# Two quarters of tokens together through three Strassen products in a hybrid decoder layer

## The chip, the cores and the metric

The kernel runs on one core of one Trainium2 chip. The metric is the device time of one execution in microseconds (us); lower is better. A core has a matrix engine (PE, with its weight loads listed as PEld), a vector engine (DVE), a scalar engine (ACT), GpSimd (POOL, hardly used here) and SyncE (SP), whose queue issues every DMA of this kernel.

## The reference

One decoder layer over 2048 tokens of width 1024, in float32. Biases, the convolutions' insides and the recurrence are left out here.

```python
h = rms_norm(x, mix_norm_g)
lru_x, lru_gate, conf_a, conf_b = split(h @ w_in, 4)            # 4 x 512
y_lru = rg_lru(causal_dwconv(lru_x, 4 taps)) * gelu(lru_gate)
c = causal_dwconv(conf_a * sigmoid(conf_b), 31 taps)
c = silu(layer_norm(c))
x = x + concat([y_lru, c]) @ w_out                              # output projection
h = rms_norm(x, xa_norm_g)
k, v = split(rms_norm(mem, mem_norm_g) @ w_kv, 2)               # 256 memory tokens, 4 heads
p = softmax((h @ w_q) . k / 16)                                 # per head
x = x + (p . v) @ w_o
h = rms_norm(x, ffn_norm_g)
g, u = split(h @ w_up, 2)                                       # 2 x 3072
x = x + (gelu(causal_dwconv(g, 3 taps)) * u) @ w_down
return rms_norm(x, final_norm_g)
```

## The kernel before

**Number format.** Each float32 operand is split into a high part `hi`, rounded for the matrix engine's fast float32 mode, and the rest `lo` (`split`: one ACT copy, one DVE subtraction). A product is three matrix multiplies, hi by hi, hi by lo and lo by hi (`mm3`). A multiply takes a 128x128 stationary and a 128x512 moving operand.

**Tokens.** The 2048 tokens are worked on in four quarters of 512 (`TT`), each of four blocks of 128 (`NTB`). Per quarter there are three tasks. `mixer(q)` does the first normalisation, the input projection, the convolutions (`conf`: 30 DVE taps for each of four channel blocks) and the recurrence (`lru`). `normed(q)` does the layer norm of the convolved half (`conf_out`). `attend(q)` does the rest up to the input of the feed-forward.

**attend(q).** It has three products with a 1024x1024 right side, each through `project_tokens`: for each half of the 1024 output columns it holds four PSUM banks, one for each token block, and adds eight k-blocks of 128 into them. The left operands lie with the contracted dimension on the partitions, so that the 128x128 pieces of them are the stationary side. The three are

- output projection: left `Y` and `L` (the two halves of the mixer's result), right `W_out`; each bank is added on DVE to the residual `xs`, and ACT squares it for the next normalisation;
- scores: left the transposed residual `xa`, right `A_rows`, which `memory_a` makes beforehand as w_q times the keys, so that h @ w_q and the keys are one product; `softmax` reads each bank (maximum on DVE, exponential and scaling on ACT), with the normalisation's factor in the exponential's scale;
- values: left the transposed probabilities `pt`, right `VO_rows`, which `memory_vo` makes as the values times w_o; again added to the residual, squared, normalised, transposed and stored in DRAM (`xn_kept`).

The right sides are kept in DRAM as hi and lo (`Rows`) and read again for each quarter.

**Feed-forward.** `up` and `Down` work on halves of 1024 tokens and use one level of Strassen's method in Winograd's form: seven products of half-size blocks in place of eight, with the sums S1 to S4 and T1 to T4 of the blocks of either side made on DVE. `HalfX` makes the combinations of the normalised tokens: `X[0]` needs quarters 0 and 1 alone, and its first five operands are made ahead by the task `first`, once `started[3]` is set. `feed_forward` (the task `tail`) waits for `attended[3]`, the end of the last values product.

**Order.** The program is written by tasks (Python generators). `drive` keeps a clock of estimated PE time and steps the first due task of the list `TURNS`, so an earlier place in the list is a higher priority; a task that yields a number comes due that many us later, one that yields a task waits for it. The constants `MIX_PACE`, `ATT_PACE` and so on are such pauses. After that `Program.schedule` orders each engine's instructions by estimated costs and due times and with a limited number of buffers (84 tiles of 128x512 in SBUF, 8 PSUM banks), given out in program order. The order of each engine and of SP's queue is then fixed in the program, and each engine runs its own in that order.

Of the kernel before, what the change touches and what calls it, by code (L numbers as in the profile page):

```python
# [417 lines left out]
def hybrid_layer(  # L418
# [41 lines left out]
    def ps():  # L460
        return pr.new("ps", name="ps")
# [347 lines left out]

    def conf_out(C, Y):  # L810
        s = block_sum(C, False)
        yield LN_SUM
        p = ps()
        matmul(p[:], ones[:], s[:], start=True, stop=True)
        for c in range(NC4):
            V("tensor_tensor", C[c][:], C[c][:], p[:], op=ALU.subtract)
        ss = block_sum(C, True)
        yield LN_SQ
        r = wide_rstd(ss, 1.0)
        for c in range(NC4):  # L820
            w = vec["v512"][:, c, :]
            V("scalar_tensor_tensor", C[c][:], C[c][:], w[:, I_LG : I_LG + 1], r[:], op0=ALU.mult, op1=ALU.mult)
            ACT(C[c][:], C[c][:], AF.Silu, bias=w[:, I_LB : I_LB + 1])
            hi, lo = pair("y")
            split(C[c][:], hi, lo)
            Y.append((hi, lo))

    def lru(q, X, L, row, pace):
        for c in (0, 2):
# [46 lines left out]
            for j in range(2):  # L876
                ge = tmp("gelu")
                ACT(ge[:], scaled("gelu", pg[j], row)[:], AF.Gelu_apprx_tanh)
                V("tensor_tensor", ge[:], H[j][:], ge[:], op=ALU.mult)
                hi, lo = pair("y")  # L880
                split(ge[:], hi, lo)
                L.append((hi, lo))
# [158 lines left out]
    started = [Task(None) for _ in range(NQ)]  # L1041
    attended = [Task(None) for _ in range(NQ)]
    x2_kept = Kept("x2", NQ * NTB * 2, F32)
    xn_kept = Kept("xn", NQ * NK, F32)
# [121 lines left out]
    def normed(q, ready, wait):  # L1166
# [4 lines left out]
        Y = []  # L1171
        yield from conf_out(C, Y)
        mixed[q] = Y, L

    def attend(q, ready):
# [24 lines left out]

        yield from turned(xs, take)
        yield mem_a
        prob = [[], []]
# [251 lines left out]
    class Down:  # L1455
# [18 lines left out]
        def operand(self, c, key, i):  # L1474
# [13 lines left out]
            return self.s[at]  # L1488

        def gather(self, c, n):  # L1490
            if (c, n) in self.ready:
# [3 lines left out]
            for i in range(KD):  # L1495
# [3 lines left out]
                L.append((hi, lo))  # L1499
                at = wd_at(c, bkey, i)  # L1500
                R.append(self.given[c, n][i] if (c, n) in self.given else (wd_kept.get(at, None, "wh"), wd_kept.get(at + 1, None, "wl")))
            self.R = R
# [23 lines left out]
        def run(self, last=None):  # L1526
            for c in self.order:
# [20 lines left out]
                if not self.h:  # L1548
# [5 lines left out]
                    self.add(pa, 1, 0)  # L1554

    def finish(h, acc):
        g = []
# [40 lines left out]
    EARLY, VO_WAIT, V_LATE, Z_COPIED = 5, 2, 500, (0, 1)  # L1598
    MIX_WAIT, MIX_TURN, LN_SUM, LN_SQ, GATES = (0, 10, 0, 0), 9, 2, 0, 4
    MIX_PACE, ATT_PACE = (1, 4, 4, 4), ((0, 4, 1), (0, 2, 6), (0, 1, 0), (0, 2, 4))  # L1600
    PAUSE = 2
    MEM_WAIT, VO_LATE, ATT_TURN, FFN_TURN, X_PACE, T_PACE = 12, 10, 1, (6, 16, 6, 100), 10, 11

    NORMED = [lambda: ([m[0]], 105), lambda: ([attended[0]], 35), lambda: ([attended[1]], 140), lambda: ([m[3], n[2]], 115)]
    ATTEND = [lambda: [n[0]], lambda: [n[1]], lambda: [n[2]], lambda: [n[3], attended[2]]]
    TURNS = lambda: [later, n[2], m[0], mem_a, m[1], n[1], n[3], a[0], n[0], mem_vo, m[2], first, a[3], a[2], a[1], m[3], first_t, tail]
    X = [HalfX(h) for h in range(NH)]
# [29 lines left out]
    for q in range(NQ):  # L1637
        m[q].gen = mixer(q, m[q - 1] if q else None)
        n[q].gen = normed(q, *NORMED[q]())
        a[q].gen = attend(q, ATTEND[q]())  # L1640
    later.gen, mem_a.gen, mem_vo.gen = setup_later(), memory_a(), memory_vo()
    first_t.gen, first.gen, tail.gen = X[0].kept(n[3], T_PACE), first_x(), feed_forward()
    tasks.extend(TURNS())
# [33 lines left out]
```

## Time and profile before

| | |
|---|---|
| Median of 3 runs | 2469.93 us (2469.36 to 2470.13) |
| The profiled execution, its own time | 2470.41 us |
| Its span, first to last instruction | 2468.5 us |
| PE busy | 2450.5 us, 99% |
| DVE busy | 1825.8 us, 74% |
| ACT busy | 1171.0 us, 47% |
| DMA | 543.70 MB, mean 220 GB/s |

In the groups of the profile a line names an engine, an operation, the tiles it writes and reads, the shapes, the count, busy time and the mean in ns of one, and the idle time just before with what ended it. Windows list a stretch, then the busy time of each engine with its number of instructions, the granted PE clock (1.00 is full), the DMA share and GB/s. Nearly all instructions carry line 394, since one function emits them all; tiles tell them apart.

### The profile page before, as it was taken

To read this page: it belongs to the slowest core of one execution; us is meant where nothing else is said; L and a number is where in the kernel's file an instruction comes from. 1 tells how busy PE (TensorE), PEld (TensorE's weight loads), DVE (VectorE), ACT (ScalarE), POOL (GpSimd) and SP (SyncE) were. 2 spreads that over 40 slices of the span, in tenths; PEclk is the share of its full clock that TensorE was granted. 3 is DMA by queue.
4 is the path that set the end of the run, shared out by engine and by line. 5 is a ranking of instruction groups with operands and counts; after the bars stand their busy time and mean duration, and the time that the engine had idled before them with its cause. 6 is when DMAs were issued, how large, how long until landed. Compare 5 with 4: busy or idle time off the path is not lost. (4 is left out here: it accounts for less than half of the span.)

```text
span 2468.5 us, 32772 instructions
## 1 busy us (share of the span) xinstructions
PE 2450.5 (99%) x11212; PEld 2037.8 (83%) x11212; DVE 1825.8 (74%) x3041; ACT 1171.0 (47%) x2041; POOL 0.7 (0%) x6
## 2 busy tenths in 40 slices
PE   9999999999999999999999999999999999999998
PEld 7898888888888788888888888888888888888887
DVE  7999993697279532369888887987886675667666
ACT  6762664366416543465545455555454432224223
POOL 0000000000000000000000000000000000000000
PEclk9999999999999999999999999999999999999999
DMA  9598676677456748777654545444542387779675
GB/s 318 209 302 320 214 256 236 214 257 257 150 174 238 250 158 293 260 254 249 234 196 151 181 165 178 166 165 163 179 145 94 120 279 263 247 253 357 234 253 177
DMA packets 327741, 543.70 MB, mean 220 GB/s; under 512 B 31580, under 2 KB 109404, under 8 KB 327574
## 3 DMA queue, kind: packets, MB, share of 16 engines
q1 hardware_dynamic: 327574, 541.60, 63.9%
q8 instruction: 89, 1.46, 0.2%
q14 instruction: 78, 0.64, 0.1%
HBM read 396.78 MB, written 144.70 MB: 219 GB/s over the span
## 5 line engine op out<-in xcount | busy, mean ns | idle before, releaser
L394 PE MATMUL ps<-Xh,wh 128*128 128x512 f32 x1344 | 523.4, 389 | 0.0
L394 PE MATMUL ps<-Xh,wl 128*128 128x512 f32 x1344 | 523.0, 389 | 0.1
L394 PE MATMUL ps<-Xl,wh 128*128 128x512 f32 x1344 | 522.9, 389 | 0.0
L394 DVE SCALAR_TENSOR_TENSOR conv<-cb,v,conv 128x512 f32<-128x512 f32 x480 | 339.6, 743 | 2.8 <-ACT conv L394 0.9
L394 PEld LDWEIGHTS ps<-Xh,wl 128*128 128x128 f32 x1344 | 252.2, 188 | 53.2 <-DVE wl L394 0.6
L394 PEld LDWEIGHTS ps<-Xh,wh 128*128 128x128 f32 x1344 | 252.3, 188 | 52.7 <-DVE up L394 0.4
L394 PEld LDWEIGHTS ps<-Xl,wh 128*128 128x128 f32 x1344 | 252.3, 188 | 52.2
L394 PE MATMUL ps<-wl,hidh 128*128 128x512 f32 x672 | 261.4, 389 | 0.0
L394 PE MATMUL ps<-wh,hidh 128*128 128x512 f32 x672 | 261.4, 389 | 0.0
L394 PE MATMUL ps<-wh,hidl 128*128 128x512 f32 x672 | 261.4, 389 | 0.0
L394 DVE TENSOR_TENSOR acc<-acc,ps 128x512 f32<-128x512 f32 x192 | 129.4, 684 | 143.8 <-PE ps L394 141.2
L394 PE MATMUL ps<-xh,wh 128*128 128x512 f32 x512 | 202.7, 396 | 0.8 <-ACT xt L394 0.8
L394 PE MATMUL ps<-xh,wl 128*128 128x512 f32 x512 | 199.4, 389 | 0.0
L394 PE MATMUL ps<-xl,wh 128*128 128x512 f32 x512 | 199.3, 389 | 0.0
L394 ACT ACTIVATE wh<-s 128x512 fp32r<-128x512 f32 x192 | 119.3, 627 | 111.9 <-DVE s L394 85.6
L394 ACT ACTIVATE wh<-raw 128x512 fp32r<-128x512 f32 x208 | 127.1, 626 | 85.0 <-PE ps L394 40.1
L394 DVE TENSOR_TENSOR wl<-raw,wh 128x512 fp32r<-128x512 f32 x208 | 141.0, 684 | 24.6 <-ACT wh L394 22.9
L394 DVE TENSOR_TENSOR wl<-s,wh 128x512 fp32r<-128x512 f32 x192 | 131.1, 686 | 29.0 <-ACT wh L394 20.2
L394 ACT ACTIVATE u<-ps 128x512 f32<-128x512 f32 x144 | 85.9, 597 | 138.9 <-PE ps L394 137.9
L394 PEld LDWEIGHTS ps<-wh,hidh 128*128 128x128 f32 x672 | 126.1, 188 | 26.2
L394 PEld LDWEIGHTS ps<-wl,hidh 128*128 128x128 f32 x672 | 126.1, 188 | 26.2
L394 PEld LDWEIGHTS ps<-wh,hidl 128*128 128x128 f32 x672 | 126.1, 188 | 26.1
(206 smaller groups left out, 4246.0 us busy)
## 6 DMA issues: line engine op xcount, KB each, us to landing
raw<-in_w_up_dram SPq DMA_DIRECT2D x96, 512.0 KB
wh<-w_down SPq DMA_DIRECT2D x164, 256.0 KB
wl<-w_down SPq DMA_DIRECT2D x164, 256.0 KB
wh<-w_in SPq DMA_DIRECT2D x96, 256.0 KB
wl<-w_in SPq DMA_DIRECT2D x96, 256.0 KB
hid<-cv SPq DMA_DIRECT2D x48, 512.0 KB
h<-hid SPq DMA_DIRECT2D x96, 256.0 KB
w_down<-wh SPq DMA_DIRECT2D x84, 256.0 KB
```

Of the source, the lines that this page charges most:

```text
L394: getattr(e, name)(*[resolve(a) for a in args], **{k: resolve(a) for k, a in kw.items()})
```

## The change

Quarters 2 and 3 (`FOLDED`) no longer have an `attend` each. A task `attend_pair` takes them together, 1024 tokens, once the layer norms of both and the attention of quarter 1 are done, and each of its three products is one level of Strassen (`Folded`, built on `Down`): seven steps of 512x512x512. The combined right sides T1 to T4 of `W_out`, `A_rows` and `VO_rows` are made by a new task `fold_weights` (`Folds`), stored in DRAM as float32, and split into hi and lo when they are read. The left operands stay in float32 and are split, plain or combined, at each step. The scores come in two parts that are added before the softmax. The factor of the second normalisation is applied before the transposes, no longer in the exponential. The residual after the output projection goes to DRAM and comes back for the values. `started[3]` is set at step 4 of the last product. The pauses and the list of priorities have new values.

```diff
-    def conf_out(C, Y):
+    def conf_out(q, C, Y):
...
+            if q in FOLDED:
+                Y.append(C[c])
+                continue
             hi, lo = pair("y")
             split(C[c][:], hi, lo)
...
                 V("tensor_tensor", ge[:], H[j][:], ge[:], op=ALU.mult)
+                if q in FOLDED:
+                    L.append(ge)
+                    continue
                 hi, lo = pair("y")
                 split(ge[:], hi, lo)
...
+    class Folds:
+
+        def __init__(self, rows, name):
+            self.rows, self.t, self.done = rows, Kept(name, 4 * KH, F32), Task(None)
+
+        def block(self, k, half):
+            if self.rows.w is not None:
+                t = tmp("wd")
+                pr.dma(t[:], self.rows.w[k * P : (k + 1) * P, half * TT : (half + 1) * TT])
+                return t
+            hi, lo = self.rows.get(k, half)
+            t = tmp("wd")
+            V("tensor_tensor", t[:], hi[:].f32(), lo[:].f32(), op=ALU.add)
+            return t
+
+        def prepare(self, wait):
+            for i in range(KH):
+                b11, b12 = self.block(i, 0), self.block(i, 1)
+                t1 = combine("t", b12[:], b11[:], ALU.subtract)
+                self.t.put(KH + i, t1[:])
+                yield wait
+                b22 = self.block(KH + i, 1)
+                t3 = combine("t", b22[:], b12[:], ALU.subtract)
+                t2 = combine("t", b22[:], t1[:], ALU.subtract)
+                self.t.put(2 * KH + i, t3[:])
+                self.t.put(i, t2[:])
+                yield wait
+                t4 = combine("t", self.block(KH + i, 0)[:], t2[:], ALU.subtract)
+                self.t.put(3 * KH + i, t4[:])
+                del b11, b12, b22, t1, t2, t3, t4
+                yield wait
+            self.done.done = True
+
+        def weight(self, key, i):
+            if key[0] == "B":
+                return self.rows.get((int(key[1]) - 1) * KH + i, int(key[2]) - 1)
+            t = self.t.get(T_KEYS.index(key) * KH + i)
+            hi, lo = pair("w")
+            split(t[:], hi, lo)
+            return hi, lo
+
+    class Folded(Down):
+
+        STEPS = (("A11", "B11"), ("A12", "B21"), ("S2", "T2"), ("S1", "T1"), ("S4", "B22"), ("S3", "T3"), ("A22", "T4"))
+
+        def __init__(self, src, folds, add):
+            self.src, self.folds, self.put = src, folds, add
+            self.raw, self.s, self.ready, self.given = {}, {}, {}, {}
+
+        def hid(self, c, kq, th, i):
+            return self.src[th, kq][i]
+
+        def weight(self, c, key, i):
+            return self.folds.weight(key, i)
+
+        def step(self, n, banks, start, into):
+            L, R = self.gather(0, n)
+            for tb in range(NTB):
+                if len(banks) == tb:
+                    banks.append(ps())
+                ts = slice(tb * P, (tb + 1) * P)
+                with together():
+                    for i in range(KH):
+                        mm3(banks[tb][:], L[i][0][:, ts], L[i][1][:, ts], R[i][0][:], R[i][1][:], start and i == 0, i == KH - 1, skip_group_check=True)
+                for th, half, last in into:
+                    self.put(th, tb, half, banks[tb], last)
+                yield 0
+
+        def run(self, before, after):
+            pa, pb, pc, pd = [], [], [], []
+            steps = (
+                (pa, True, ((0, 0, False),)),
+                (pb, True, ((0, 0, True),)),
+                (pa, False, ((0, 1, False),)),
+                (pc, True, ((1, 1, False),)),
+                (pc, False, ((0, 1, True),)),
+                (pa, False, ((1, 1, True), (1, 0, False))),
+                (pd, True, ((1, 0, True),)),
+            )
+            for n, (banks, start, into) in enumerate(steps):
+                yield from before(n)
+                yield from self.step(n, banks, start, into)
+                after(n)
+
+    def attend_pair(ready):
+        for t in ready:
+            yield t
+        q0 = FOLDED[0]
+        me = a[q0]
+        src = {}
+        x1_kept = Kept("x1", 4 * NTB, F32)
+
+        def nothing(n):
+            return ()
+
+        def residual(load, store, st):
+            acc = {}
+
+            def add(th, tb, half, bank, last):
+                at = (th, tb, half)
+                if at not in acc:
+                    acc[at] = load(th, tb, half)
+                t = acc[at]
+                V("tensor_tensor", t[:], t[:], bank[:], op=ALU.add)
+                if last:
+                    st[th].add(tb, half, t[:])
+                    store(th, tb, half, t)
+
+            return acc, add
+
+        def normalise(acc, th, st, wait, take):
+            yield wait
+            r = st[th].rstd()
+            ys = []
+            for tb in range(NTB):
+                row = []
+                for half in range(2):
+                    t = tmp("xn")
+                    ACT(t[:], acc[th, tb, half][:], AF.Copy, scale=r[:, tb : tb + 1])
+                    row.append(t)
+                ys.append(row)
+            yield PAIR_TURN
+            yield from turned(ys, take)
+
...
+        def after1(n):
+            if n in (4, 6):
+                th = n // 6
+                posts[th] = spawn(normalise(acc, th, st1, PAIR_WAIT[0], take_xa(th)), me)
+
+        yield F_out.done
+        yield from Folded(src, F_out, add).run(nothing, after1)
+        del acc, add
+
+        yield mem_a
+        yield F_a.done
+        psrc, score = {}, {}
+        prob = {}
+        turns = []
+
+        def soften(th, tb, half, bank, last):
+            at = (th, tb, half)
+            if not last:
+                t = score[at] = tmp("score")
+                ACT(t[:], bank[:], AF.Copy)
+                return
+            t = score.pop(at)
+            V("tensor_tensor", t[:], t[:], bank[:], op=ALU.add)
+            prob.setdefault((th, half), []).append(softmax(t, M ** -0.5, -(M ** -0.5)))
+
+        def turn_raw(th, half):
+            yield PAIR_WAIT[1]
+            for j in range(4):
+                p = ps()
+                with together():
+                    for tb in range(NTB):
+                        transpose(p[:, tb * P : (tb + 1) * P], prob[th, half][tb][:, j * P : (j + 1) * P], ident[:])
+                t = tmp("pt")
+                ACT(t[:], p[:], AF.Copy)
+                psrc.setdefault((th, half), []).append(t)
+                if j % 2:
+                    yield 0
+
+        def before2(n):
+            if n == 0:
+                yield posts[0]
+            if n == 2:
+                yield posts[1]
+
+        def after2(n):
+            for at in {4: ((0, 0), (0, 1)), 5: ((1, 1),), 6: ((1, 0),)}.get(n, ()):
+                turns.append(spawn(turn_raw(*at), me))
+
+        yield from Folded(xsrc, F_a, soften).run(before2, after2)
...
+        def before3(n):
+            if n == EARLY_AT:
+                started[NQ - 1].done = True
+            if n == 0:
+                yield turns[0]
+            if n == 1:
+                yield turns[1]
+            if n == 2:
+                yield turns[2]
+                yield turns[3]
+
+        def after3(n):
+            if n in (4, 6):
+                th = n // 6
+                finals.append(spawn(normalise(acc2, th, st2, PAIR_WAIT[2 + th], take_xn(th)), me))
+
+        yield from Folded(psrc, F_vo, add2).run(before3, after3)
+        for th in range(2):
+            attended[q0 + th].done = True
+        for t in finals:
+            yield t
+
+    def fold_weights():
+        for f, ready, wait in zip((F_out, F_a, F_vo), FOLD_AT(), FOLD_PACE):
+            for t in ready:
+                yield t
+            yield from f.prepare(wait)
+
     EARLY, VO_WAIT, V_LATE, Z_COPIED = 5, 2, 500, (0, 1)
-    MIX_WAIT, MIX_TURN, LN_SUM, LN_SQ, GATES = (0, 10, 0, 0), 9, 2, 0, 4
-    MIX_PACE, ATT_PACE = (1, 4, 4, 4), ((0, 4, 1), (0, 2, 6), (0, 1, 0), (0, 2, 4))
+    MIX_WAIT, MIX_TURN, LN_SUM, LN_SQ, GATES = (1, 13, 0, 0), 6, 7, 1, 4
+    MIX_PACE, ATT_PACE = (0, 4, 6, 4), ((0, 3, 0), (0, 0, 6), (7, 1, 1), (4, 0, 6))
     PAUSE = 2
-    MEM_WAIT, VO_LATE, ATT_TURN, FFN_TURN, X_PACE, T_PACE = 12, 10, 1, (6, 16, 6, 100), 10, 11
-
-    NORMED = [lambda: ([m[0]], 105), lambda: ([attended[0]], 35), lambda: ([attended[1]], 140), lambda: ([m[3], n[2]], 115)]
-    ATTEND = [lambda: [n[0]], lambda: [n[1]], lambda: [n[2]], lambda: [n[3], attended[2]]]
-    TURNS = lambda: [later, n[2], m[0], mem_a, m[1], n[1], n[3], a[0], n[0], mem_vo, m[2], first, a[3], a[2], a[1], m[3], first_t, tail]
+    MEM_WAIT, VO_LATE, ATT_TURN, FFN_TURN, X_PACE, T_PACE = 0, 11, 1, (5, 0, 17, 5), 6, 2
+
+    FOLDED = (2, 3)
+    PAIR_WAIT, PAIR_TURN, FOLD_PACE = (1, 0, 9, 15), 5, (15, 6, 40)
+    EARLY_AT = 4
+    FOLD_AT = lambda: ([turned_x[0]], [mem_a, turned_x[1]], [mem_vo])
+    F_out, F_a, F_vo = Folds(W_out, "t_out"), Folds(A_rows, "t_a"), Folds(VO_rows, "t_vo")
+
+    NORMED = [lambda: ([m[0]], 111), lambda: ([attended[0]], 33), lambda: ([m[2]], 2), lambda: ([m[3], n[2]], 0)]
+    ATTEND = [lambda: [n[0]], lambda: [n[1]]]
+    TURNS = lambda: [later, m[0], first_t, m[3], n[1], first, mem_a, fold, m[1], a[0], n[0], mem_vo, m[2], n[2], n[3], a[1], a[2], tail]
...
-        a[q].gen = attend(q, ATTEND[q]())
+        if q not in FOLDED:
+            a[q].gen = attend(q, ATTEND[q]())
+    a[3] = a[2]
+    a[2].gen = attend_pair([n[2], n[3], attended[1]])
+    fold = Task(fold_weights())
     later.gen, mem_a.gen, mem_vo.gen = setup_later(), memory_a(), memory_vo()
-    first_t.gen, first.gen, tail.gen = X[0].kept(n[3], T_PACE), first_x(), feed_forward()
+    first_t.gen, first.gen, tail.gen = X[0].kept(a[1], T_PACE), first_x(), feed_forward()
```

More of the change, by code (lines that the diff above doesn't have):

```diff
@@ L1042, in hybrid_layer @@
     attended = [Task(None) for _ in range(NQ)]
+    turned_x = [Task(None) for _ in range(NQ)]
     x2_kept = Kept("x2", NQ * NTB * 2, F32)
@@ L1171, in normed @@
         Y = []
-        yield from conf_out(C, Y)
+        yield from conf_out(q, C, Y)
         mixed[q] = Y, L
@@ L1201, in attend @@
         yield from turned(xs, take)
+        turned_x[q].done = True
         yield mem_a
@@ L1488, in operand @@
             return self.s[at]
+        def weight(self, c, key, i):
+            at = wd_at(c, key, i)
+            return wd_kept.get(at, None, "wh"), wd_kept.get(at + 1, None, "wl")
         def gather(self, c, n):
@@ L1499, in gather @@
                 L.append((hi, lo))
-                at = wd_at(c, bkey, i)
-                R.append(self.given[c, n][i] if (c, n) in self.given else (wd_kept.get(at, None, "wh"), wd_kept.get(at + 1, None, "wl")))
+                R.append(self.given[c, n][i] if (c, n) in self.given else self.weight(c, bkey, i))
             self.R = R
@@ L1554, in run @@
                     self.add(pa, 1, 0)
+    T_KEYS = ("T2", "T1", "T3", "T4")
+    class Folds:
[34 more added lines that the diff above has]
+            return hi, lo
@@ new lines, in hybrid_layer, with weight @@
+    class Folded(Down):
[5 more added lines that the diff above has]
+            return self.src[th, kq][i]
+        def weight(self, c, key, i):
+            return self.folds.weight(key, i)
[26 more added lines that the diff above has]
+                after(n)
@@ new lines, in attend_pair, with load_one, operands, take_xa @@
+    def attend_pair(ready):
[32 more added lines that the diff above has]
+            yield from turned(ys, take)
+        def load_one(th, tb, half):
+            t = tmp("x1")
+            r0 = (q0 + th) * TT + tb * P
+            pr.dma(t[:], x[0, r0 : r0 + P, half * TT : (half + 1) * TT])
+            return t
+        def operands(th):
+            Y, L = mixed[q0 + th]
+            src[th, 0], src[th, 1] = L, Y
+        operands(0)
+        operands(1)
+        st1 = [Stats(), Stats()]
+        acc, add = residual(load_one, lambda th, tb, half, t: x1_kept.put((th * NTB + tb) * 2 + half, t[:]), st1)
+        xsrc, posts = {}, [None, None]
+        def take_xa(th):
+            def take(k, p):
+                t = tmp("xa")
+                ACT(t[:], p[:], AF.Copy, scale=vec["v1024"][:, k, G_XA : G_XA + 1])
+                xsrc.setdefault((th, k // KH), []).append(t)
+            return take
+        def after1(n):
[40 more added lines that the diff above has]
+        yield from Folded(xsrc, F_a, soften).run(before2, after2)
+        xsrc.clear()
+        yield mem_vo
+        yield F_vo.done
+        st2 = [Stats(), Stats()]
+        acc2, add2 = residual(
+            lambda th, tb, half: x1_kept.get((th * NTB + tb) * 2 + half, None, "acc"),
+            lambda th, tb, half, t: x2_kept.put(((q0 + th) * NTB + tb) * 2 + half, t[:]),
+            st2)
+        finals = []
+        def take_xn(th):
+            def take(k, p):
+                t = tmp("xt")
+                ACT(t[:], p[:], AF.Copy, scale=vec["v1024"][:, k, G_FFN : G_FFN + 1])
+                xn_kept.put((q0 + th) * NK + k, t[:])
+            return take
+        def before3(n):
[17 more added lines that the diff above has]
+            yield t
```

## The prediction

> **What bounds the kernel now.** I read the page first (busy shares, the slices), then busy time by stages, then the matrix-multiply groups, then what PE waited for.
>
> ```profile
> PE 2450.5 (99%) x11212; PEld 2037.8 (83%) x11212; DVE 1825.8 (74%) x3041; ACT 1171.0 (47%) x2041; POOL 0.7 (0%) x6
> PE   9999999999999999999999999999999999999998
> DVE  7999993697279532369888887987886675667666
> ACT  6762664366416543465545455555454432224223
> PEclk9999999999999999999999999999999999999999
> ```
> ```profile
> 0.00:100.00 100.00, 94.70 (x461) 79.96 (x462) 81.60 (x169) 68.28 (x121) 0.70 (x6) 1.00 0.87 304
> 100.00:350.00 250.00, 249.01 (x1244) 212.95 (x1243) 245.41 (x417) 139.91 (x238) 0.00 (x0) 1.00 0.78 267
> 350.00:600.00 250.00, 249.65 (x1179) 207.46 (x1179) 180.99 (x315) 133.17 (x237) 0.00 (x0) 1.00 0.68 230
> 600.00:830.00 230.00, 226.27 (x1054) 187.06 (x1053) 159.67 (x277) 118.33 (x217) 0.00 (x0) 1.00 0.61 210
> 830.00:1095.00 265.00, 264.31 (x1240) 219.58 (x1239) 104.12 (x190) 116.04 (x264) 0.00 (x0) 1.00 0.68 238
> 1110.00:2010.00 900.00, 899.97 (x3971) 744.83 (x3970) 739.39 (x1150) 448.67 (x687) 0.00 (x0) 1.00 0.51 173
> ```
>
> Columns: window, length, busy time of PE, PEld, DVE, ACT, POOL, granted clock, DMA share, GB/s. PE is the bound from end to end: idle 18 us of 2468.5, only 0.7 us of it between 830 and 1095, where the last two quarters attend. DVE is full in bursts (the convolutions of the mixers) and 39% busy from 830 to 1095; ACT is 44% there. A change must take matrix work from PE, or it gains nothing; what it adds to DVE and ACT is free only while PE has something else to do.
>
> **What a multiply costs.**
>
> ```profile
> L394 PE MATMUL ps<-wh,yh 128*128 128x512 f32 x256 | 100.3, 392 | 0.0
> L394 PE MATMUL ps<-wh,xah 128*128 128x512 f32 x256 | 100.1, 391 | 0.0
> L394 PE MATMUL ps<-wh,pth 128*128 128x512 f32 x256 | 101.2, 395 | 0.3
> ```
> ```profile
> 1003.00:1028.00 25.00, 25.00 (x112) 1.00 0.64 196
> ```
>
> The groups are the output projection (y), the scores (xa) and the values (pt), each the first of three terms (high by high, high by low, low by high). So each product has 768 multiplies, 192 for a quarter. Their mean of 390 ns is not what one costs: in the stage from 1110 to 2010, 3971 fit into 899.97 us, 0.2266 us each, and a stretch of attention (25 us, 112) goes at the same pace. The records overlap; the pitch is the price.
>
> The Trainium skill (TensorE: Matmul & The Clock Gate, "Wait — 56ns, not 53.3ns?") gives the start-to-start time of a warm multiply as N / 2.4 GHz plus about 2.5 ns, 215.7 ns at N = 512. By it the multiplies saved below would be worth 31.1 us and not 32.6; the trace's pitch is 5% longer, so I use the trace.
>
> **The change part by part.** *PE, removed.* Two quarters by the plain form: 2 x 192 = 384 multiplies for a product. By one level of Strassen: 7 steps x 4 token blocks x 4 k-blocks x 3 terms = 336. Three products: 3 x 48 = 144 fewer, 144 x 0.2266 = **32.6 us off PE**. Transposes stay the same in number (16 groups of four for a quarter's two normalisations, 8 for its probabilities).
>
> *DVE and ACT, added.*
>
> ```profile
> L394 DVE TENSOR_TENSOR x<-x,ps 128x512 f32<-128x512 f32 x64 | 43.5, 683 | 83.4 <-PE ps L394 81.8 <-DMA wh<-A 1.3
> L394 DVE TENSOR_REDUCE smalls<-ps 128x2 f32<-128x512 f32 x32 | 22.0, 688 | 86.4 <-PE ps L394 86.4
> 1243.45 0.68 DVE L394 TENSOR_TENSOR up<-u,ps 128x512 f32<-128x512 f32 x1
> 1244.05 0.68 DVE L394 TENSOR_TENSOR wl<-s,wh 128x512 fp32r<-128x512 f32 x1
> 1246.37 0.62 ACT L394 ACTIVATE wh<-raw 128x512 fp32r<-128x512 f32 x1
> 1246.89 0.62 ACT L394 ACTIVATE wh<-s 128x512 fp32r<-128x512 f32 x1
> 991.58 3.59 ACT L394 ACTIVATE xah<-ps,v 128x512 fp32r<-128x512 f32 x6
> 1014.51 0.56 ACT L394 ACTIVATE prob<-ps,smalls 128x256 f32<-128x256 f32 x1
> 1015.05 0.56 ACT L394 ACTIVATE prob<-ps,smalls 128x256 f32<-128x256 f32 x1
> 1018.15 2.92 ACT L394 ACTIVATE prob<-prob,smalls 128x256 f32<-128x256 f32 x7
> 1012.11 1.28 ACT L394 ACT_TABLE_LOAD   x1 [15.18 <-DVE smalls L394]
> L394 ACT ACTIVATE junk<-x 128x512 f32<-128x512 f32 x32 | 20.3, 636 | 69.6 <-DVE x L394 69.3
> 602.70 3.65 PE L394 MATMUL ps<-ident,x 128*128 128x128 f32 x32
> ```
>
> Pitches again: 0.60 us for a DVE tensor-tensor, 0.52 for an ACT copy, 0.60 for one with a scale, 0.54 for an exponential with its sum read, 0.42 for a half-width copy, 0.64 for a square (its mean), 0.46 for four transposes. DVE gains: folds of the weights 16 + 32 + 32 = 80 (the A and VO blocks must first be summed from their halves); S1 to S4, 16 for a product, 48; left operands 84 low parts instead of 48, +36; combined weights split when read, 48; and 48 additions, since a bank goes to 8 places and not 4 for each token block (16 each in the first and last product, 16 scores added in place of read from PSUM). 260 x 0.60 = 156 us. ACT gains 36 + 48 high parts, 16 copies each of scores, of probabilities and of xa, and 16 scalings before the first transposes: 148, about 79 us.
>
> *What of it stands beside the pair.* The pair is 1008 x 0.2266 = 228 us of multiplies and 48 transpose groups, 22 us: 250 us of PE. Beside it ACT has 84 + 48 splits (69 us), 32 squares (20), 64 scaled copies (38), 32 plain copies (17), 32 exponentials (17), 32 half-width copies (13), some 6 table loads (8), and 20 splits for the feed-forward's first operands, now released at step 4 of the last product (10): 193 us, 77%. DVE has 84 + 48 + 48 + 80 at 0.60, 16 reductions, 20 splits: some 185 us, 74%. Neither is the bound over the whole pair; both were under half before. So the added work costs nothing by volume, and the cost lies at the joints, where no other matrix work exists: the feed-forward waits for the last quarter, and quarters 0 and 1 are done.
>
> *Joint 1, out to scores.* From the last bank of a half: add 0.6, square 0.64, root with table load 1.6, reciprocal and sum 0.3, eight scalings 4.8, transposes 0.46, eight copies 4.8, S1 and S2 1.2, split 1.1: 15.5 us, some 18 with the hops. Cover: two steps of 48 multiplies, 21.7 us (steps 5 and 6 for the first half, steps 0 and 1 of the scores for the second). ACT's work in those four steps and 16 transpose groups (50.8 us): 42 us. It fits, with the queue's order against it. Bounds 0 and 12; I take 3.
>
> *Joint 2, scores to values.* Step 2 of the values needs all four probability tiles of each block; the last is finished after step 6. Chain of its last tile: add 0.6, reduction 0.7, exponentials 1.1, copies 0.8, transposes and copies 2.5, combination and split 2.3: 8 us, cover 21.7. But ACT has to do in these four steps three of the four softmax groups (3 x 8 x 0.96 = 23), 24 splits (12.5), 16 copies of turned probabilities (8.3), 4 score copies (2), two loads (2.6): 48 of 50.8 us. Full, with a strict order. Bounds 0 and 15; I take 5.
>
> *Start and end.* The layer norm of quarter 3 now stands ahead of step 2 of the pair. Its sums left PE idle before:
>
> ```profile
> PE ps L394 <- DVE sum L394: 1.7, 1, 1.7
> PE ps L394 <- ACT xt L394: 0.8, 1, 0.8
> ```
>
> Attention of quarter 1 is the filler, at low priority. Bounds 0 and 10; I take 2. At the end, five operands of the feed-forward have to be loaded and split in three steps (32.6 us) with 26 us of ACT work; bounds 0 and 5, I take 2. The last normalisations run into the feed-forward, whose ACT is 50% busy: nothing.
>
> *SP and DMA.*
>
> ```profile
> wh<-A SPq DMA_DIRECT2D x64, 256.0 KB
> wh<-VO SPq DMA_DIRECT2D x64, 256.0 KB
> wh<-w_out SPq DMA_DIRECT2D x48, 256.0 KB
> ```
>
> Two quarters read 192 weight tiles (32 for a product, high and low); the pair reads 120 (24 plain, 16 combined, for each). Folding adds 80 reads and 48 writes, and the residual goes out and back, 32: net 88 tiles of 0.26 MB, 23 MB more in 1080 us, against 0.61 to 0.87 of DMA share. They are placed one at a time on SP between loads; a write waits for its DVE result and holds the loads behind it. Bounds 0 and 5; I take 0, as that share leaves room.
>
> Sum on the profiled execution (2470.4 us, span 2468.5, 0.5 above the median of 2469.9): -32.6 + 3 + 5 + 2 + 2, less the 0.7 idle of the old stage, gives **2449 us**, about 0.8% less. Less than 0.2% (5 us) I count as no change.
>
> **Rivals.** *A: all joints covered.* For it: PE idled 0.7 us in the old stage with the same kind of chains. Then 32.6 and up to 4 of the idle before 830 are saved: 2434 to 2443. Chance 0.21.
>
> *B: ACT is the bound at both joints.* Joint 2 stands at 48 of 50.8 us before any order is lost. If both joints go to their upper bounds, 27 us, with 4 at start and end, 2468: no change, or a little better. Chance 0.13.
>
> *C, the other side: quarter 3 is late.* Before, attention of quarter 2 began at 826 us with quarter 3 behind it; the pair needs quarter 3 at its third step. The work ahead is that of the first 828 us, in which DVE was busy 81.6 + 245.4 + 181.0 + 159.7 = 668. To it come the folds (48), the layer norm of quarter 3 and the early combinations for the feed-forward (25), less 10 for splits that go: 731 of 828. The idle 97 suffices only if it isn't left in holes as before:
>
> ```profile
> 825.59 0.50 PE L394 MATMUL ps<-wh,yl 128*128 128x512 f32 x1 [0.38 <-DVE yl L394]
> 400.00:450.00 50.00, 50.00 (x238) 41.79 (x238) 10.40 (x24) 14.26 (x35) 0.00 (x0) 1.00 0.62 201
> 600.00:650.00 50.00, 50.00 (x240) 41.93 (x239) 15.38 (x38) 31.54 (x78) 0.00 (x0) 1.00 0.42 148
> 650.00:700.00 50.00, 49.18 (x248) 40.93 (x246) 17.11 (x30) 19.02 (x41) 0.00 (x0) 1.00 0.65 217
> ```
>
> These three windows leave 107 us idle. If the old idle (160) stays, quarter 3 ends at about 891, 63 late, 41 after the two steps that cover it: 2490. Slower from about 97 + 22 + 20 = 139 us of DVE idle on. Against it: new priorities put mixer 3 ahead. Chance 0.17.
>
> *D: gaps cool PE.* The trace's tail shows it: PE's last multiply ends at 2461.7.
>
> ```profile
> 2461.00:2464.00 3.00, 0.68 (x3) 0.21 (x2) 1.66 (x4) 2.42 (x8) 0.00 (x0) 1.00 0.45 175
> 2464.00:2468.50 4.50, 0.00 (x0) 0.00 (x0) 0.92 (x2) 0.74 (x2) 0.00 (x0) 0.62 0.61 233
> ```
>
> A mean of 0.62 fits half speed from some 3.4 us after the end. If each of four joints has one gap longer than that, and takes as long to warm as to cool, each costs 1.7 us more: 2456. Chance 0.06. The Trainium skill (the same page, "Why this matters for your kernels") has it as a rule: no gaps over about 3 us between bursts. No gap of the trace before is followed by slow multiplies, so only the tail bears it out.
>
> **How the numbers follow.** The forecast, joints of 5 to 25 us (2443 to 2463), has 0.43; A 0.21, B 0.13 (half of it above 2465), C 0.17, D 0.06. The range 2435 to 2474 leaves out C and the outermost of A. Faster: 0.43 + 0.21 + 0.06 + 0.06 = 0.76; within 0.2% 0.07 and a little of C, 0.09; slower 0.15. The likeliest alone has 2443 to 2463.
>
> **What would show it.** PE's multiplies 144 fewer, DVE about 150 us and ACT about 75 us busier, all before the feed-forward, which should start some 20 us earlier than at 1095. PE idle of 10 to 15 us in the 250 us before that, mostly ahead of the third step of scores and values and released by ACT. Wrong if PE waits there for DVE on quarter 3's conv or layer norm (C), if idle exceeds 30 us (B), or if the multiplies fall by another number.

## The result and the profile after

| | median us | lowest to highest | runs | ratio to before, 95% interval |
|---|---|---|---|---|
| before | 2470.03 | 2469.36 to 2470.45 | 4 | |
| changed | 2456.27 | 2455.17 to 2458.45 | 4 | 0.9946, 0.9928 to 0.9963 |

The profiled execution of the changed kernel took 2455.91 us with a span of 2454.1, 14.4 us shorter than before. The kernel is faster, by 13.8 us. The forecast was 2449, so 7 us of the gain are missing. The lines of the page that answer to those shown of before:

```profile
PE 2422.9 (99%) x11068; PEld 2014.0 (82%) x11068; DVE 1974.7 (80%) x3297; ACT 1248.6 (51%) x2189; POOL 0.7 (0%) x6
PE   9999999999999799999999999999999999999998
DVE  7999994399789978879888788987886675667656
ACT  6762665335925678685545445555454431225223
PEclk9999999999999899999999999999999999999999
DMA packets 340416, 566.78 MB, mean 231 GB/s; under 512 B 32988, under 2 KB 110812, under 8 KB 340246
```

PE has 144 instructions fewer. One slice, the fourteenth (797 to 859 us), has fallen to 7 tenths, and the granted clock falls with it. Busy time by the same stages (columns: window, its length, busy time of PE, PEld, DVE, ACT and POOL with the number of instructions, granted clock, DMA share, GB/s):

```profile
0.00:100.00 100.00, 96.08 (x465) 81.32 (x465) 82.61 (x170) 68.12 (x120) 0.70 (x6) 1.00 0.85 298
100.00:350.00 250.00, 248.81 (x1242) 212.12 (x1241) 244.92 (x415) 143.98 (x242) 0.00 (x0) 1.00 0.78 268
350.00:600.00 250.00, 249.83 (x1194) 207.37 (x1193) 176.45 (x307) 114.69 (x222) 0.00 (x0) 1.00 0.78 270
600.00:830.00 230.00, 210.88 (x942) 171.62 (x941) 206.60 (x359) 137.07 (x233) 0.00 (x0) 0.96 0.79 274
830.00:1095.00 265.00, 265.00 (x1269) 222.39 (x1268) 218.73 (x391) 201.28 (x430) 0.00 (x0) 1.00 0.72 242
```

From 830 to 1095, where the three Strassen products of the pair stand, PE is never idle, although DVE is 83% busy and ACT 76%. The loss lies before: from 600 to 830 PE idles 19.1 us, where it idled 3.7. What PE waited for, in total, times and longest us:

```profile
PE ps L394 <- DVE sum L394: 11.6, 1, 11.6
PE ps L394 <- DMA raw<-in_ffn_norm_g_dram: 3.4, 1, 3.4
PE ps L394 <- DVE xl L394: 2.2, 3, 1.3
PE ps L394 <- ACT xn L394: 2.0, 4, 1.1
PE ps L394 <- DMA wh<-VO: 1.9, 1, 1.9
PE ps L394 <- ACT prob L394: 1.8, 3, 0.9
```

The first row was 1.7 us before, for a layer norm of quarter 2. It is one wait now, for the sum of squares in the layer norm of quarter 3. The timeline of PE around it (start and duration in us, then what was idle ahead of it in brackets):

```profile
810.16 1.02 PE L394 MATMUL ps<-sum,ones 128*128 128x512 f32 x2
822.83 2.04 PE L394 MATMUL ps<-sum,ones 128*128 128x512 f32 x2 [11.65 <-DVE sum L394]
823.89 1.41 PE L394 MATMUL ps<-wh,hidh 128*128 128x512 f32 x1
825.10 0.63 PE L394 MATMUL ps<-wl,hidh 128*128 128x512 f32 x1
...
828.39 0.40 PE L394 MATMUL ps<-wh,hidh 128*128 128x512 f32 x1
```

The layer norm's first sum goes at 810, right behind the last input projection of quarter 3. Then come the subtraction of the mean, the squares and their addition on DVE and ACT, and the second sum at 823. The next instruction in PE's order is step 0 of the pair. PE has nothing in between. In the kernel before, the two sums of quarter 3 (the same view) stand here:

```profile
920.39 1.02 PE L394 MATMUL ps<-sum,ones 128*128 128x512 f32 x2
928.09 1.02 PE L394 MATMUL ps<-sum,ones 128*128 128x512 f32 x2
```

There the layer norm of quarter 3 came over 100 us later, in the midst of the attention of quarter 2, and PE waited for neither sum. Quarter 2's own layer norm had 16 us between its two sums, and PE idled for only 1.7 of them, because the output projection of the same quarter began in between:

```profile
796.38 1.02 PE L394 MATMUL ps<-sum,ones 128*128 128x512 f32 x2
799.99 0.39 PE L394 MATMUL ps<-wh,yh 128*128 128x512 f32 x1
812.72 1.12 PE L394 MATMUL ps<-sum,ones 128*128 128x512 f32 x2 [1.69 <-DVE sum L394]
```

Those multiplies use the recurrence's half `L`, which needs no layer norm. Step 0 of the pair likewise uses `L` of quarter 2 alone, yet in the changed kernel it stands behind the second sum. Its operands are also late: DVE finishes the last low part of them just ahead of that sum,

```profile
821.38 0.70 DVE L394 TENSOR_TENSOR hidl<-gelu,hidh 128x512 fp32r<-128x512 f32 x1
```

so no bank of step 0 could have been finished in the gap. DVE is never idle there. Only seven of its instructions between the two sums (four subtractions of the mean and three additions of squares, 4.2 us at 0.60) belong to the layer norm. The others are the recurrence, the operands of step 0 and early combinations for the feed-forward.

### The profile page after: what moved, and what is told of

Same layout as the page of the kernel before. It is cut to its first block, busy times and chain, and to the rows that moved or that the text cites. A ratio compares the mean times of both kernels' runs of the same rounds, so it can differ in the third digit from the quotient of the medians.

```text
span 2454.1 us, 33077 instructions
## 1 busy us (share of the span) xinstructions
PE 2422.9 (99%) x11068; PEld 2014.0 (82%) x11068; DVE 1974.7 (80%) x3297; ACT 1248.6 (51%) x2189; POOL 0.7 (0%) x6
## 5 line engine op out<-in xcount | busy, mean ns | idle before, releaser
L394 PE MATMUL ps<-wh,hidh 128*128 128x512 f32 x1008 | 394.2, 391 | 0.0
L394 PE MATMUL ps<-wl,hidh 128*128 128x512 f32 x1008 | 392.9, 390 | 0.0
L394 PE MATMUL ps<-wh,hidl 128*128 128x512 f32 x1008 | 392.8, 390 | 0.0
L394 DVE TENSOR_TENSOR acc<-acc,ps 128x512 f32<-128x512 f32 x224 | 151.0, 687 | 152.3 <-PE ps L394 149.6
L394 PEld LDWEIGHTS ps<-wh,hidh 128*128 128x128 f32 x1008 | 189.7, 188 | 39.9 <-ACT gelu L394 0.5
L394 PEld LDWEIGHTS ps<-wl,hidh 128*128 128x128 f32 x1008 | 189.6, 188 | 39.7 <-issue 0.5
L394 PEld LDWEIGHTS ps<-wh,hidl 128*128 128x128 f32 x1008 | 189.6, 188 | 39.5
L394 ACT ACTIVATE hidh<-s 128x512 fp32r<-128x512 f32 x144 | 87.8, 630 | 189.1 <-DVE s L394 134.3
```

Of the source, the lines that this page charges most:

```text
L394: getattr(e, name)(*[resolve(a) for a in args], **{k: resolve(a) for k, a in kw.items()})
```

## The experiments

All times are medians beside runs of the kernel before on the same chip. Those runs gave 2470.2 us for the first four experiments, 2469.99 for the next four and 2469.93 for the last two. The first four ask where the loss comes from.

**late3: the pair waits for quarter 3 only ahead of its step 2.**

```diff
-        operands(1)
+        def before1(n):
+            if n == 2:
+                yield normeds[q0 + 1]
+                operands(1)
...
-        yield from Folded(src, F_out, add).run(nothing, after1)
+        yield from Folded(src, F_out, add).run(before1, after1)
...
-    a[2].gen = attend_pair([n[2], n[3], attended[1]])
+    a[2].gen = attend_pair([n[2], attended[1]])
```

> The pair no longer waits for quarter 3 before its first step, but before its third; nothing else is edited (the planner then orders all engines anew). Theory 'order': the 11.6 us idle ahead of the pair and the slow multiplies behind it exist only because the whole pair stands behind quarter 3's layer norm in PE's order; steps 0 and 1 (21.7 us of PE) need quarter 2 alone and fill the gap: 14 us gained, about 2442 us, no idle over 4 us near the start of the pair. Rival 'volume': DVE is full up to 885 us, so the missing DVE time shows as a wait at step 2 in place of step 0: less than 4 us gained, 2452 us or more.

Measured: 2467.5 us (2465.45 to 2471.69), ratio 0.9991 (0.9982 to 0.9999): 11 us slower than the changed kernel. PE's largest wait is as long as in the changed kernel and has moved behind steps 0 and 1:

```profile
PE ps L394 <- ACT hidh L394: 12.0, 1, 12.0
```

The two steps that I had counted as a cover (22 us) don't help here. Once they go first, the rest of quarter 3 is later by as much: its second sum goes at 843.44 instead of 822.83. Behind it PE waits for the operands of step 2, a wait that steps 0 and 1 covered in the changed kernel. So the wait in the task isn't the cause. 'Order' is refuted; the sign of 'volume', a wait at step 2, is there, but neither of the two expected a loss.

**late3x: the same, and X[0]'s operands wait for quarter 3's layer norm, as before.**

```diff
-    first_t.gen, first.gen, tail.gen = X[0].kept(a[1], T_PACE), first_x(), feed_forward()
+    first_t.gen, first.gen, tail.gen = X[0].kept(n[3], T_PACE), first_x(), feed_forward()
```

> As late3, and the feed-forward's early combinations (X[0]) wait for quarter 3's layer norm again, as in the kernel before; that takes some 5 us of DVE out of 800 to 830 us. Theory 'order': DVE's volume there no longer decides, the same as late3 within 2 us. Rival 'volume': another 3 to 5 us less than late3.

Measured: 2464.06 us (2460.9 to 2464.81), ratio 0.9972 (0.9961 to 0.9983), with one wait of 13.3 us for `hidh`. Same picture, 3.4 us better, as 'volume' had it: which operations stand on DVE ahead of quarter 3's layer norm does count.

**nofold: the 80 DVE operations of `Folds` are left out.**

```diff
-                b11, b12 = self.block(i, 0), self.block(i, 1)
-                t1 = combine("t", b12[:], b11[:], ALU.subtract)
-                self.t.put(KH + i, t1[:])
+                b11, b12 = self.raw(i, 0), self.raw(i, 1)
+                self.t.put(KH + i, b11)
...
```

> The arithmetic that makes T1 to T4 is left out (80 DVE additions, 48 us); blocks of the right sides are stored in their place, so the result isn't the reference's; reads, writes and all later work stay. Theory 'order': nearly all folds run before 700 us, where DVE had idle time, so little comes of it: 2452 to 2456 us. Rival 'volume': the folds are what makes quarter 3 late, 10 us or more gained, 2446 us or less.

Measured: 2454.96 us (2453.44 to 2456.55), ratio 0.9938 (0.9926 to 0.9951). DVE is busy 1927.3 us instead of 1974.7, 47 less, and the time falls by 1.3, less than the two spreads. The second sum goes 7 us earlier, after a gap of 9.0, but PE then waits again between 840 and 860 (busy 17.11 of 20). The folds cost next to nothing, as the prediction had it.

**plainnew: the new pauses and priorities, with all four quarters attended in the plain form.**

```diff
-    FOLDED = (2, 3)
+    FOLDED = ()
...
-    ATTEND = [lambda: [n[0]], lambda: [n[1]]]
+    ATTEND = [lambda: [n[0]], lambda: [n[1]], lambda: [n[2], attended[1]], lambda: [n[3], attended[2]]]
...
```

> The new pauses and priorities alone: all four quarters attend by the plain products, no folds, no pair. My theory: the gain comes from the 144 multiplies and not from the pauses: 2465 to 2480 us. Rival: the new pauses are worth something themselves, 2462 us or less.

Measured: 2490.18 us (2489.32 to 2492.28), ratio 1.0082 (1.0069 to 1.0096). Busy time by windows:

```profile
750.00:800.00 50.00, 45.23 (x204) 36.83 (x202) 47.89 (x87) 36.97 (x55) 0.00 (x0) 0.97 0.72 256
800.00:850.00 50.00, 42.44 (x166) 33.48 (x167) 37.05 (x61) 29.86 (x46) 0.00 (x0) 0.90 0.94 343
```

This splits the change in two, as far as equal pauses make an equal order (each kernel is planned anew). With them Strassen's form is worth 2490.2 - 2456.3 = 33.9 us (worked out: 32.6). Without it the pauses and priorities cost 20 us by themselves, 10 more than the upper end of my range. PE idles 12.3 us in these 100 us (before: 2.9), and the granted clock falls. It is the same stretch as in the changed kernel and not the same wait: the longest is 4.9 us for an operand of the gates, and the second sum of quarter 3 isn't waited for.

The next three ask what holds quarter 3 back, and whether the joints inside the pair were really free.

**fewtaps: the last 10 of 30 DVE taps of quarter 3's convolution are left out, with the order of every engine kept.**

```diff
...
+                    if t >= taps:
+                        pr.ops[-1].calls.clear()
...
-        yield from conf(X, C, pb, row, MIX_PACE[q])
+        yield from conf(X, C, pb, row, MIX_PACE[q], CK if q < 3 else 21)
```

> The last 10 of the 30 DVE taps are left out in each of quarter 3's four channel blocks (40 instructions, 26 us of DVE inside the stretch from 690 to 830 in which DVE is full), so the result isn't the reference's; the order of every engine stays that of the changed kernel. Theory 'volume' (quarter 3's DVE burst ends too late): PE's gap of 11.65 us ahead of the second layer-norm sum falls under 4 us, its small waits on DVE from 770 to 805 go, and the multiplies behind it run at full pace: 12 to 18 us gained on the changed kernel, 2438 to 2444 us. Rival 'chain' (the sums, subtractions and squares that follow PE's last independent work take that long whatever DVE did before): the gap stays over 8 us, 2452 us or more.

Measured: 2456.11 us (2455.01 to 2457.56), ratio 0.9944 (0.9931 to 0.9956): nothing gained. Windows, and below them the second sum in PE's timeline:

```profile
780.00:790.00 10.00, 9.05 (x39) 7.28 (x40) 2.30 (x4) 9.94 (x15) 0.00 (x0) 0.83 0.83 288
810.00:820.00 10.00, 2.52 (x10) 1.41 (x8) 10.00 (x17) 9.97 (x18) 0.00 (x0) 0.78 1.03 369
```
```profile
823.64 2.04 PE L394 MATMUL ps<-sum,ones 128*128 128x512 f32 x2 [11.12 <-DVE sum L394]
```

DVE now has time to spare ahead (2.30 us busy of 10 from 780 to 790), and the sum still goes at 824, as the rival 'chain' said. It comes some 12 us behind the end of quarter 3's input projection on PE, whose last multiplies start at about 811 here and 810 in the changed kernel. In these 12 us the recurrence, the layer norm and the operands of step 0 stand in one order on DVE, which is full (10.00 of 10 from 810 to 820). DVE's volume ahead of the two sums is not it.

**warm: 45 multiplies of constants, 128x128, stand on PE ahead of the second sum.**

```diff
...
+        pr.ops[-1].calls[:0] = [("matmul", (p[:, :P], ones[:], ident[:]), dict(start=True, stop=True))] * extra
...
-        r = wide_rstd(ss, 1.0)
+        r = wide_rstd(ss, 1.0, 45 if q == 3 else 0)
```

> 45 small multiplies of constants (128x128, about 0.22 us each, 10 us in all) are issued on PE just ahead of quarter 3's second layer-norm sum; they need nothing that is late, and nothing else is edited, so that PE is busy in the gap. Theory 'gaps cool PE': the nine multiplies behind the gap (0.43 us apart in place of 0.227) and the sum itself run at full pace, granted clock 1.0 from 820 to 830, 2 to 4 us gained on the changed kernel: about 2453 us. Rival 'the slow multiplies are slow for their operands' sake': pace unchanged, 2456 us.

Measured: 2458.3 us (2457.71 to 2458.56), ratio 0.9952 (0.9939 to 0.9964): no gain. It is 2 us above the changed kernel, with ratio intervals that overlap. Timeline of PE:

```profile
812.93 10.21 PE L394 MATMUL ps<-ident,ones 128*128 128x128 f32 x90
824.65 1.12 PE L394 MATMUL ps<-sum,ones 128*128 128x512 f32 x2 [1.51 <-DVE sum L394]
849.88 0.50 PE L394 MATMUL ps<-wl,hidh 128*128 128x512 f32 x1 [1.42 <-DVE wl L394]
```

The 10 us of multiplies fill the gap and the sum goes at full pace (1.12 us instead of 2.04). The 2 us are not their doing: the profiled execution is 1.9 us later before them, since the first sum goes at 812.07 instead of 810.16. From there to the first multiply of the feed-forward both kernels take 262.4 us (to 1074.49 here, to 1072.57 in the changed kernel). So the 2.6 us that the full pace saves (worked out below) are lost again; 1.9 of them can be seen as new waits for weights split on DVE, from 849 on. The slow multiplies are a symptom here.

**actmore: three more half-width ACT copies behind each of the 16 softmax tiles of the pair, some 20 us of ACT.**

```diff
+            pr.ops[-1].calls.extend([("activation", (prob[th, half][-1][:, M:], prob[th, half][-1][:, M:], AF.Copy), {})] * 3)
```

> Three more half-width ACT copies (in place, values unchanged) behind each of the pair's 16 softmax tiles, order otherwise that of the changed kernel: 48 x 0.42 = 20 us of ACT, 15 us of it between step 4 of the scores and step 2 of the values. The prediction's step 'joint 2 is full, 48 of 50.8 us': PE idles 8 us or more there, 2464 us or more. Rival 'slack' (work is spread ahead of the joint, none of it was exposed, so the term was mis-sized because it was counted into too short a window): PE idle in the pair stays under 2 us, 2456 to 2458 us.

Measured: 2476.6 us (2474.99 to 2478.25), ratio 1.0027 (1.0017 to 1.0037): 20.3 us slower for 19.8 us of ACT (1248.6 to 1268.4 busy). What PE waited for between 940 and 1060 us, and its busy time there:

```profile
PE ps L394 <- ACT prob L394: 7.5, 5, 3.5
PE ps L394 <- DVE score L394: 2.5, 1, 2.5
PE ps L394 <- ACT pt L394: 1.9, 3, 1.6
```
```profile
960.00:980.00 20.00, 14.51 (x70) 11.54 (x69) 14.79 (x31) 19.01 (x51) 0.00 (x0) 0.91 0.47 155
980.00:1000.00 20.00, 16.27 (x74) 13.20 (x72) 13.20 (x28) 19.35 (x53) 0.00 (x0) 0.94 0.91 318
1000.00:1020.00 20.00, 17.35 (x70) 13.81 (x71) 12.34 (x26) 18.28 (x48) 0.00 (x0) 0.81 0.44 141
```

In the changed kernel PE waits for nothing in that stretch. Of the 20.3 us, 11.9 are these waits. About 7 more are pace: the granted clock is 0.91, 0.94 and 0.81 in the three windows, and PE's busy time is 6.8 us above that of the changed kernel. The waits fit the count of 48 of 50.8 us of ACT work at joint 2: of the 15 us that were to fall into the joint 2.8 would fit, and 12.2 would not. The joint is nearly full and not over. That the total is so close to the ACT time added is chance.

**tuned: other pauses and priorities for the same work.**

```diff
...
-    MEM_WAIT, VO_LATE, ATT_TURN, FFN_TURN, X_PACE, T_PACE = 0, 11, 1, (5, 0, 17, 5), 6, 2
+    MEM_WAIT, VO_LATE, ATT_TURN, FFN_TURN, X_PACE, T_PACE = 0, 11, 1, (9, 6), 6, 2
...
-    PAIR_WAIT, PAIR_TURN, FOLD_PACE = (1, 0, 9, 15), 5, (15, 6, 40)
+    PAIR_WAIT, PAIR_TURN, FOLD_PACE = (1, 1, 10, 15), 5, (15, 6, 40)
...
-    TURNS = lambda: [later, m[0], first_t, m[3], n[1], first, mem_a, fold, m[1], a[0], n[0], mem_vo, m[2], n[2], n[3], a[1], a[2], tail]
+    TURNS = lambda: [later, m[0], first_t, first, mem_a, fold, m[1], a[0], n[0], mem_vo, m[3], n[1], m[2], n[2], n[3], a[1], a[2], tail]
...
-    first_t.gen, first.gen, tail.gen = X[0].kept(a[1], T_PACE), first_x(), feed_forward()
+    first_t.gen, first.gen, tail.gen = X[0].kept(n[3], T_PACE), first_x(), feed_forward()
```

> The changed kernel with other pauses and priorities: the feed-forward's early combinations wait for quarter 3's layer norm, mixer 3 and the layer norm of quarter 1 stand lower in the list, and small pauses differ. Theory 'order ahead of quarter 3': the gap ahead of the pair shrinks to 6 to 8 us, 2449 to 2452 us. Rival: what is taken out there comes back as waits elsewhere, 2455 us or more.

Measured: 2452.12 us (2450.02 to 2452.78), ratio 0.9927 (0.9913 to 0.994), the fastest version here and 4 us better than the changed kernel. PE's wait for the sum is down to 1.2 us; the largest is now

```profile
PE ps L394 <- DVE x L394: 8.5, 2, 7.4
```

ahead of 837 us. Steps 0 and 1 run from 805 on, partly between the two sums; step 2 adds into step 0's banks and has to wait until DVE has read them, and that addition stands behind quarter 3's last operations. The time is at the upper end of the theory's range, and the rival's waits elsewhere are there as well.

**xlate and turnsonly: the two halves of that, one at a time.** The first has only the edit of `X[0].kept`, the second all the others.

> The changed kernel with one edit: the first half of the feed-forward's operands may be made once quarter 3's layer norm is planned, not only once quarter 1's attention is. Theory 'operands' (the 4 us that the retimed kernel gains over the changed one, 2452.1 to 2456.3, come from this: fewer operations of the feed-forward stand in DVE's and ACT's order ahead of quarter 3's layer norm): 2451 to 2453 us, the gap ahead of the second layer-norm sum well under 11.65 us. Rival 'turns' (they come from the order of the tasks, which puts quarter 3's last input projection at 804.5 instead of 809.9 us): 2455 to 2457, the gap as in the changed kernel.

> The changed kernel with the other edits of the retimed one: quarter 3's mixer and quarter 1's layer norm stand behind the memory's second task in the order of turns, and two pauses differ (FFN_TURN of quarters 0 and 1, PAIR_WAIT). Theory 'turns' (quarter 3's last input projection goes earlier, and the chain behind it with it): 2451 to 2453 us, the last of those multiplies at about 804 us. Rival 'operands': 2455 to 2457 us, the last of them at about 810 and a gap of some 11 us behind it.

Measured: xlate 2453.4 us (2452.16 to 2455.8), ratio 0.9935 (0.9922 to 0.9949); turnsonly 2460.72 (2459.64 to 2461.14), ratio 0.9961 (0.9949 to 0.9974). The two sums of quarter 3 in xlate, with the first and the last multiply of step 0 between them, and DVE's low parts for step 0:

```profile
806.76 1.02 PE L394 MATMUL ps<-sum,ones 128*128 128x512 f32 x2
810.38 0.39 PE L394 MATMUL ps<-wh,hidh 128*128 128x512 f32 x1
818.31 0.40 PE L394 MATMUL ps<-wh,hidl 128*128 128x512 f32 x1
818.54 1.02 PE L394 MATMUL ps<-sum,ones 128*128 128x512 f32 x2
```
```profile
805.90 2.49 DVE L394 TENSOR_TENSOR hidl<-gelu,hidh 128x512 fp32r<-128x512 f32 x4
```

In xlate the gap is gone. The chain is hardly shorter (11.8 us between the sums instead of 12.7); it is covered. With the early combinations held back, DVE has the operands of step 0 ready at 808.4 instead of 822.1, and 36 of that step's 48 multiplies stand ahead of the second sum. PE is idle 11.8 of the 300 us from 600 to 900, in waits of 1.9 us at most, against 19.1 in the changed kernel. 'Operands' holds for the gap. For the time the evidence is weaker: the median is 0.4 us outside the forecast range, and runs and ratio intervals of xlate and the changed kernel overlap a little. 'Turns' is refuted: those edits alone cost 4.5 us, with the gap of 11.5 still there and the last of the input projections at 809. That they give a little on top of the other edit (1.3 us, ranges overlapping) isn't shown.

Of the gap's 11.65 us little comes back as time. New short waits and slow multiplies stand in its place: over the whole span PE idles 6.1 us less than in the changed kernel, and is busy 3.6 us longer.

## Why the prediction was right, and where it was off

Everything happens ahead of the feed-forward. Its first multiply starts here before and after:

```profile
1086.09 0.39 PE L394 MATMUL ps<-Xh,wh 128*128 128x512 f32 x1
```
```profile
1072.57 0.39 PE L394 MATMUL ps<-Xh,wh 128*128 128x512 f32 x1
```

That is 13.5 us earlier, for 13.8 in the time. In tuned it is 1066.82, in late3 1084.97. The forecast had "some 20 us earlier".

*The work removed and added: right.* 144 multiplies fewer were forecast and counted. They were priced at 32.6 us, and plainnew against the changed kernel gives 33.9. DVE was to be about 150 us busier and is 148.9, ACT 75 and is 77.6, DMA 23 MB and is 23.08. Folds cost next to nothing (nofold). PE's largest wait on a transfer, 3.4 us for the feed-forward's norm weights, stands in all these kernels. The row of 1.9 us for `wh<-VO` is new; xlate has a wait of the same length at the same place (658 to 660 us) put down to DVE, so whether the added DMA causes it isn't shown. Beside the pair DVE's list adds up to 179 us and not to "some 185"; from 830 to 1095 it was busy 83% where 74 were counted, ACT 76 where 77 were.

*The joints: over-sized.* Joint 1 was taken as 3 us, joint 2 as 5, the end as 2. All three are 0, since PE has no idle time from 830 to 1095. Rival A had this right. The idle time was forecast ahead of the third steps of scores and values, released by ACT; it came ahead of the first step of the pair, released by DVE. At joint 2 only the size was off: actmore shows that it has little to spare.

*The start: the step that failed.* It was taken as 2 us with 10 as its upper bound. PE's idle time from 600 to 830 rose from 3.7 to 19.1, 15.4 us more. Three things in that step were wrong. The row of 1.7 us was read as quarter 3's layer norm; it is quarter 2's (812.72 in the kernel before). Attention of quarter 1 was named as the filler, but its last product ends at 762 us. And what does fill such a chain, the first multiplies of the next output projection, was missed: rival C has attention of quarter 2 begin at 826 us, while its multiplies start at 799.99, ahead of the second sum. C's two steps as a cover were right in kind, but in the changed kernel the sum stands ahead of step 0 in PE's order, so they cover only what comes behind the sum. In xlate step 0 stands ahead and the gap is gone. In late3 both steps stand ahead of the second sum, step 0 even ahead of quarter 3's last projections, and PE waits 12 us behind the sum instead. The sign that the text gave for C, PE waiting for DVE on quarter 3's layer norm, came true just ahead of the pair, though not its price. DVE was idle for 830 - (82.6 + 244.9 + 176.5 + 206.6) = 119 us before 830, between the 97 that suffices and the 139 at which the kernel would have been slower.

*Rival D, in part.* After the 11.65 us gap the first multiplies run at a pitch of 0.43 us until 828.3. From 822.83 to 825.10 the sum and the first multiply take 2.27 us instead of warm's 1.20 (824.65 to 825.85), and the next eight multiplies take 3.29 instead of 1.81: 2.6 us, where D had 1.7 for each gap. The Trainium skill (TensorE: Matmul & The Clock Gate, "Why this matters for your kernels") asks for no gap over about 3 us; the trace agrees, with one gap of 11.65 us and the half pace behind it. Shorter gaps are not always safe, though. In xlate, after waits of 1.53, 0.80 and 0.77 us between 822 and 827, the same pitch of 0.43 us lasts from 827.75 to 832.87:

```profile
827.75 0.63 PE L394 MATMUL ps<-wh,hidh 128*128 128x512 f32 x1
832.44 0.63 PE L394 MATMUL ps<-wh,hidl 128*128 128x512 f32 x1
```

That the kernel's time would come back with the pace is not borne out by warm.

*What was luck.* The forecast is only 7 us off because errors of both signs met. The joints and the end were taken 10 us too high. The start was taken 13.4 too low, and 5 us of PE's busy time were not foreseen (nor 1.4 us gained at the kernel's start). With the joints alone put right the forecast would have been 2439, 17 us off.

The account by the two spans: -32.6 for the multiplies, +13.2 of PE idle (31.2 us instead of 18.0; the 15.4, less 0.7 in the pair and 1.4 at the kernel's start), and +5 of PE busy time, since it fell by 27.6 and not by 32.6. That is -14.4, the difference measured. Of the 5 us 2.6 are the half pace behind the gap. Some 1.5 more stand from 780 to 784, where the granted clock is 0.83 and twelve transposes take 2.47 us instead of 1.4. The rest isn't traced.

*What stays open.* Which limit keeps quarter 3's projection and chain from going earlier: the 84 buffers given out in program order, or the order of DVE and PE that the plan makes. xlate points to the second, and plainnew shows that the new pauses and priorities cost time without any pair. DVE's volume ahead of the chain is excluded (fewtaps, nofold), and so are the wait in the task (late3) and the clock (warm). No run puts step 0 ahead of the second sum and edits nothing else, and more buffers weren't tried.

## What to carry to other kernels

When two pieces of work are joined to save matrix time, ask what the engine has to do while the last input of the joined piece is being finished, and whether that work stands ahead of the wait in the fixed order with its operands ready. Here the joined piece itself had such work, and it stood behind. The arithmetic saved 33.9 us, and the new pauses and priorities gave 20 back. A test that keeps these and undoes the arithmetic separates the two at once. A joint that a count shows as full (48 of 50.8 us) can still cost nothing, but then little more may be put there.

## What the runs showed of the hardware

Small multiplies are enough to keep the matrix engine's pace: 90 records of 128x128 in 10.21 us (warm) held the clock at 1.00 (the first two rows) through a stretch where the changed kernel was granted 0.73 and 0.59 (the last two):

```profile
810.00:820.00 10.00, 10.00 (x76) 9.13 (x75) 10.00 (x19) 9.50 (x17) 0.00 (x0) 1.00 0.98 327
820.00:830.00 10.00, 8.49 (x51) 7.07 (x50) 10.00 (x17) 7.46 (x10) 0.00 (x0) 1.00 1.04 386
810.00:820.00 10.00, 1.18 (x4) 0.31 (x2) 10.00 (x17) 8.78 (x16) 0.00 (x0) 0.73 1.02 354
820.00:830.00 10.00, 7.17 (x18) 5.05 (x19) 10.00 (x16) 6.25 (x7) 0.00 (x0) 0.59 1.03 398
```

After the gap half pace lasted 5.5 us of dense work, from 822.83 to 828.3, longer than the some 3.4 us that the prediction worked out for its fall at the kernel's end. Half pace also followed three waits of 1.5, 0.8 and 0.8 us within 5 us (xlate), while one wait of 1.7 us in the kernel before left the clock at full (812.72; 1.00 from 812 to 820). And an engine that is 51% busy over the whole kernel passed on 19.8 us of extra work as 20.3 us of time (actmore), because most of it fell into one stretch that was nearly full: 11.9 us of waits, and about 7 us of lower clock with them.
